# A hybrid decoder layer on one core: slots claimed early for the last w2 weights, two w_ob blocks between w_oa blocks, and FFN b's first weights in weight tiles

## The chip, the cores and the metric

The kernel runs on one core of a Trainium2 chip. Its metric is the time of one execution on the device in microseconds, less is better. Before the change it was 2166.63 us, the median of 3 runs (2165.53 to 2170.79).

## The reference

One layer of a decoder runs over 1056 token rows (1024 of a prompt, 32 of eight samples), model width 1024, hidden width 2816, all in float32:

```
h = layer_norm(ALPHA * x + 0.5 * swiglu(x, f1_w1, f1_w3, f1_w2), ln1_g, ln1_b)
z = h @ w_in + b_in
...
att = combine_groups(outs, lses).astype(h.dtype)
yb, vrows = sgu_branch(uv, sgu_ln_g, sgu_ln_b, sgu_ws, sgu_b)
mix = (jax.nn.sigmoid(ga) * (att @ w_oa) + jax.nn.sigmoid(gb) * (yb @ w_ob)) @ w_out
h = layer_norm(ALPHA * h + mix, ln2_g, ln2_b)
h = layer_norm(ALPHA * h + 0.5 * swiglu(h, f2_w1, f2_w3, f2_w2), ln3_g, ln3_b)
```

`swiglu(x, w1, w3, w2)` is `(silu(x @ w1) * (x @ w3)) @ w2`. `att` (256 wide) comes from three groups of windowed attention, `yb` (512 wide) from a gated chunk mixing. The two FFNs are called FFN a and FFN b below.

## The kernel before, in words

**Products.** Every matrix product is made of TensorE matmuls of 128x128 weights by 264 tokens (four token chunks c of 264 make 1056). A float32 value is split into a high part, a copy that ScalarE casts (L250), and a low part, the difference that VectorE takes (L251); `mm3` issues three matmuls for each 128-deep step (high by high, high by low, low by high), all at L239. Results stand in PSUM in two kinds of tiles, "mm" (three buffers) and "ax" (five). A product may start only when VectorE has taken the result of the product that held its tile before: of an mm tile, that is the third product ahead. Taking it is called evacuation here.

**Weights.** `unit` (L214 on) fetches a weight block of 128x1024 into a raw tile R (L218; two buffers), casts and splits it into two tiles, from the weight pool W (eight buffers) or, with slot=True, from the general pool of S tiles (37 slots). `narrow` does the same for a half or quarter block, both parts in one W tile. Behind each fetch stands a copy of a piece of state from DRAM to DRAM (L211), on the same queue, SyncE's. The order of the instructions is found by a scheduler that runs through the program text with priorities; what comes into a pool's tile later waits until its former content has been read for the last time.

**The end of an FFN.** Most of an FFN's hidden blocks run through Strassen-like sums with seven products; the last part, `out`, walks over g = 0..2 and np = 0..3 with blocks of w2, each prepared by `prep` (L376): it fetches two raw tiles, then yields between steps in which sums of the blocks are formed and split; the last step takes two S tiles, h34 and l34 (L402). A `held` tile (L103) is an S tile that is claimed at once by a one-column copy on GpSimd (L107). During the last block (`final`), each of the seven products calls `fetch`, which loads the hidden blocks of four "plain" blocks, already split, from DRAM scratch (partA or partB, L762, eight tiles of 128x1056), and `W2` collects the fetched w2 units for them. Then the plain products follow, per output block n and token chunk c: twelve matmuls each (L920 is the evacuation), with layer norm steps between (L527 to L549 the centring, L588 to L598 the squares, L626 the scaling, L539 and L540 sums for the mean).

**mix.** After attention, `local(n)` makes w_ob block n: four products of twelve matmuls, each result multiplied into the gate `mt[n]` (L1577). All eight run first. Then eight w_oa blocks: four products of six matmuls each, multiplied into `ta[n]` (also L1577), `mt[n] += ta[n]` over all tokens (L1685), and a split of the sum. Beside blocks 2, 4 and 5 one more gate block of matmuls runs on TensorE. `column_sums` runs between on VectorE (L1643).

**From mix into FFN b.** The w_out products (blocks 3 to 7 for each of four chunks, evacuated at L1702) are followed by a layer norm whose result is written to scratch hD (L643) and split into the operands of FFN b. FFN b starts with plain hidden blocks; for i = 2, `plain` holds two of them. The two units of the first are fetched at c == 2 into S slots, the units of the second when FFN b begins, into W tiles.

Of the kernel before, what the change touches and what calls it, by code (L numbers as in the profile page):

```python
# [13 lines left out]
F32R = mybir.dt.float32r  # L14
# [7 lines left out]
P = 128  # L22
# [11 lines left out]
NG = SEVEN // GP  # L34
HP = GP * P
ORDER = (1, 2, 6, 7, 5, 4, 3)
PLAIN = (0, 19, 20, 21)
NPL = len(PLAIN)
NW = 2
# [30 lines left out]
NLEAD = 6  # L70
NTAIL = 10
LAST = 3
BESIDE = {2: 13, 4: 14, 5: 15}
CHUNKED = 3
SPLIT = [*QKV, 22, 23, 24, 25, 18, 19, 20, 21, *GATES[NLEAD : 16 - NTAIL]]
# [5 lines left out]
class Trunk:  # L81
# [285 lines left out]
    def prep(self, src, f, H, engine):  # L367

        nc = self.nc
        lo, hi, n = slice(0, H), slice(H, 2 * H), 2 * H  # L370
        with self.tc.high_priority(offset=URGENT):
            ab, cd = self.R([P, D])[:, :n], self.R([P, D])[:, :n]
            nc.sync.dma_start(ab, src[1])
            dma = nc.sync.dma_start(cd, src[0])
        self.copy_state(dma, 2)
        tt = engine.tensor_tensor  # L376
        ah, al = self.W([P, D]), self.W([P, D])
        self.split(ah[:, :n], al[:, :n], ab)
        yield
        s12 = self.Q([P, D])  # L380
        tt(s12[:, lo], cd[:, lo], cd[:, hi], op=ALU.add)  # L381
        tt(s12[:, hi], s12[:, lo], ab[:, lo], op=ALU.subtract)  # L382
        yield
        s34 = self.Q([P, D])
        h12, l12 = self.W([P, D]), self.W([P, D])
        self.split(h12[:, :n], l12[:, :n], s12[:, :n])
        tt(s34[:, lo], ab[:, lo], cd[:, lo], op=ALU.subtract)
        yield
        tt(s34[:, hi], ab[:, hi], s12[:, hi], op=ALU.subtract)  # L389
        part = lambda h, l, o=0: [((h, l), o + k * P) for k in range(H // P)]  # L390
        if n == D:
            dd = self.S([P, D], F32R)
            self.split(dd[:, lo], dd[:, hi], cd[:, hi])
            p4 = part(dd[:, lo], dd[:, hi])
        else:
            p4 = []
            for h, l, w in ((ah, al, D - n), (h12, l12, H - (D - n))):
                o = H + len(p4) * P
                self.split(h[:, n : n + w], l[:, n : n + w], cd[:, o : o + w])
                p4 += part(h, l, n)[: w // P]  # L400
        yield
        h34, l34 = self.S([P, D], F32R), self.S([P, D], F32R)  # L402
        self.split(h34[:, :n], l34[:, :n], s34[:, :n])
        self.L[f] = {
            1: part(ah, al), 2: part(ah, al, H), 5: part(h12, l12), 6: part(h12, l12, H),
            7: part(h34, l34), 3: part(h34, l34, H), 4: p4,
        }
        yield
# [260 lines left out]
    def ffn(self, w13, w2p, w2, i, mode, resid):  # L669
# [29 lines left out]
                        next(preps[x] if x == 1 else x, None)  # L699
            self.bg.extend((s0, s1))  # L700
        else:
            units, s1 = self.early
            lns, self.lns = self.lns, {}
            self.drain(lns[NC - 2])
            self.step(self.bg, 1)
            lead = [units] + [[self.unit(w13[f, x]) for x in range(2)] for f in plain[1:]]
            begin(1)
            for c in range(NC):
                self.drain(lns.pop(c))
# [3 lines left out]
                for f, u in zip(plain, lead):  # L713
                    self.hidden8(u, f, c)
                    if c:
                        with self.chained():
                            next(preps[1], None)
            lead = None
        self.sqs = {}
        self.Y = self.A = None  # L720
        loads = deque(self.load_sums(resid))
# [838 lines left out]
    def mix(self):  # L1560
# [99 lines left out]
        self.sums = sums = column_sums()  # L1660
        self.slow.append(sums)
        wbs = deque([self.narrow(a["wo"][0, :, 2 * P :], 4 * P)])
        for n in range(KB):
            local(n)
        was = deque([self.narrow(a["wo"][0, :, : 2 * P], 2 * P)])
        self.yb = None
        ta = [self.fetch_z(26 + n) for n in range(3)]
        while self.bg or self.mid or self.slow[0] is not sums:
            self.tick(1, 1 if self.slow[0] is not sums else 0)
# [3 lines left out]
        for n in range(KB):  # L1673
            wa = was.popleft()
            if n + 1 < KB:
                was.append(self.narrow(a["wo"][n + 1, :, : 2 * P], 2 * P))
            if n + 3 < KB:
                m = NLEAD + NTAIL - KB + n + 3
                ta.append(kept[m] if m in kept else self.fetch_z(29 + n))
            if 26 + n in LATE_GATES:  # L1680
                nc.scalar.activation(ta[n], ta[n], AF.Sigmoid)
            for c in range(NC):
                product(wa, att, c, ta[n])
                self.tick(0, 1)
            nc.vector.tensor_tensor(mt[n], mt[n], ta[n], op=ALU.add)  # L1685
            m2.append((self.S([P, NT], F32R), self.S([P, NT], F32R)))
            self.split(*m2[n], mt[n])
            done += 1
            if n in BESIDE:
                gate(BESIDE[n], NC - 1, 0, 0)  # L1690
        units = kept = self.A = None
        self.sqs, self.lns = {}, {}
        self.Y = self.new_Y(self.hD[0])

# [21 lines left out]
                    centers.append(self.center(c, hs, REST))  # L1716
                    self.mid.append(centers[c])
        ws = [self.unit(a["wout"][n], slot=n < KB - 4) for n in range(half, KB)]
        self.T, self.L = ({}, {}), {}
        self.normed = [None] * NC  # L1720
        for c in range(NC):
            self.drain(centers[c])
# [2 lines left out]
                self.square_step(c, n)  # L1725
            for n in range(half, KB):
                block(ws[n - half], n, c)
            self.start_ln(c, 1, "spill")
            if c == 2:
                units = [self.unit(a["w13b"][0, x], slot=True) for x in range(2)]  # L1730
                self.drain(self.lns[1])
                self.slow.append(self.spread(0, self.Y, self.normed, nc.vector))
        hs = self.hs = None
        self.A = self.normed
        self.early = units, self.spread(1, self.Y, self.normed, nc.vector)

    def run(self):
        a = self.a
# [159 lines left out]
```

## Time and profile before

| what | value |
|---|---|
| median of 3 runs | 2166.63 us |
| the profiled execution | 2166.3 us, of which the span is 2164.2 us |
| mean granted TensorE clock | 0.995 of full speed |
| TensorE busy | 2126.6 us of the span |
| VectorE busy | 1551.9 us |
| ScalarE busy | 889.0 us |
| GpSimd busy | 325.2 us |

In a row of a timeline stand the start, the duration, the engine (PE is TensorE, DVE VectorE, ACT ScalarE, SP SyncE and its DMA queue), the line, the operation, the output and the inputs by pool name, the shape, and how many such instructions the row joins; in brackets how long the engine had been idle before it, and what ended that. The end of a matmul is modelled, so the time lost at a wait is better read from start to start, less the products between. A row of the stretches shows the stretch and its length, then the busy time of PE, PEld, DVE, ACT and POOL with the number of instructions, the granted clock, the DMA share and GB/s.

### The profile page before, as it was taken

How to read it: one execution, taken by the hardware profiler on the slowest of the kernel's cores; microseconds unless marked ns; L12 is line 12 of the kernel's file. 1: busy time of each engine (PE TensorE's matmuls, PEld its weight loads, DVE VectorE, ACT ScalarE, POOL GpSimd, SP SyncE). 2: the span in 40 equal slices, each digit the busy share in tenths (PEclk: the TensorE clock that was granted, in tenths of full speed). 3: DMA queues.
4: the chain of work that ended last, by engine and by line, in shares of the span. 5: the costliest groups of instructions: out<-in, count | busy, mean ns of one | idle time of the engine just before them, and what ended most of it. 6: DMA issues, size and time to landing. Idle time of an engine off the chain costs nothing.

```text
span 2164.2 us, 43247 instructions
## 1 busy us (share of the span) xinstructions
PE 2126.6 (98%) x17307; PEld 2087.7 (96%) x17307; DVE 1551.9 (72%) x2727; ACT 889.0 (41%) x1680; POOL 325.2 (15%) x245
## 2 busy tenths in 40 slices
PE   9999999999999999999999999999999999999997
PEld 8999999999998999999998889999999999999997
DVE  8777777746788835787766658778667777657887
ACT  5444444421224634434475543255444444421224
POOL 0432332200000012222000000000223233100000
PEclk9999999999999999999999999999999999999998
DMA  4445545598875335666865665424444554596852
GB/s 160 146 137 165 190 156 169 202 345 316 330 275 192 130 114 174 208 227 207 289 215 165 217 191 173 154 86 133 138 169 155 189 165 160 192 408 267 305 189 81
DMA packets 168377, 426.51 MB, mean 197 GB/s; under 512 B 24352, under 2 KB 59792, under 8 KB 165488
## 3 DMA queue, kind: packets, MB, share of 16 engines
q1 hardware_dynamic: 167744, 423.21, 56.1%
q8 instruction: 135, 2.21, 0.4%
q14 instruction: 66, 0.54, 0.1%
q10 hardware_dynamic: 432, 0.54, 0.1%
HBM read 304.31 MB, written 165.57 MB: 217 GB/s over the span
## 4 chain that ended last, share of the span: by engine, by line
PE 89%; DVE 5%; DMA 4%; ACT 1%; issue 1%; POOL 0%; SPq 0%; ACTq 0%; DVEq 0%; POOLq 0%
PE ax L239 47%; PE mm L239 38%; PE ax L1201 1%; DMA S<-zD 1%; PE ax L1248 1%; PE ax L1225 1%; DVE W L251 1%; DVE S L251 1%; DMA S<-cD 0%; DMA M<-kv 0%; DVE S L1577 0%; DMA R<-wz 0%; DVE S L626 0%; DMA R<-w2a 0%; PE ax L1543 0%
## 5 line engine op out<-in xcount | busy, mean ns | idle before, releaser
L239 PE MATMUL ax<-S,W 128*128 128x264 f32 x5400 | 706.6, 284 | 1.8 <-ACT S L1029 1.5
L239 PE MATMUL mm<-S,W 128*128 128x264 f32 x5208 | 693.5, 287 | 13.6 <-DVE S L1577 4.1
L239 PEld LDWEIGHTS mm<-S,W 128*128 128x128 f32 x5208 | 655.2, 189 | 27.6 <-issue 8.5
L239 PEld LDWEIGHTS ax<-S,W 128*128 128x128 f32 x5400 | 676.5, 188 | 4.6 <-ACT S L1029 3.0
L239 PE MATMUL ax<-S,S 128*128 128x264 f32 x3240 | 475.7, 284 | 1.6 <-ACT S L1029 1.1
L239 PEld LDWEIGHTS ax<-S,S 128*128 128x128 f32 x3240 | 427.8, 188 | 2.3 <-ACT S L1029 1.3
L239 PE MATMUL mm<-S,S 128*128 128x264 f32 x2472 | 385.2, 286 | 2.6 <-DVE S L251 2.0
L239 PEld LDWEIGHTS mm<-S,S 128*128 128x128 f32 x2472 | 335.1, 189 | 4.3 <-DVE S L251 2.2
L250 ACT CAST W<-R 128x1024 fp32r<-128x1024 f32 (+3 forms) x173 | 128.6, 761 | 317.3 <-PE mm L239 149.9
L381 POOL TENSOR_TENSOR Q<-R 128x512 f32<-128x512 f32 x49 | 73.4, 1498 | 794.1 <-DMA R<-wz 176.8
L251 DVE TENSOR_TENSOR W<-R,W 128x1024 fp32r<-128x1024 f32 (+3 forms) x173 | 156.5, 908 | 23.9 <-ACT W L250 22.9
L250 ACT CAST W<-Q 128x1024 fp32r<-128x1024 f32 (+1 forms) x78 | 76.8, 985 | 213.9 <-POOL Q L382 86.8
L815 DVE SCALAR_TENSOR_TENSOR S<-ax,S 128x264 f32<-128x264 f32 x240 | 99.4, 427 | 66.9 <-PE ax L239 66.5
L456 DVE TENSOR_TENSOR S<-ax,M 128x264 f32<-128x264 f32 x82 | 32.6, 432 | 149.2 <-PE ax L239 149.2
L251 DVE TENSOR_TENSOR S<-Q,S 128x1024 fp32r<-128x1024 f32 (+1 forms) x78 | 108.5, 1391 | 3.8 <-ACT S L250 3.8
L251 DVE TENSOR_TENSOR W<-Q,W 128x1024 fp32r<-128x1024 f32 (+1 forms) x78 | 89.9, 1153 | 27.2 <-ACT W L250 27.2
L250 ACT CAST S<-Q 128x1024 fp32r<-128x1024 f32 (+1 forms) x78 | 76.7, 984 | 68.3 <-PE ax L239 49.8
L107 POOL CAST S<-ones 128x1 fp32r<-128x1 f32 x32 | 17.6, 570 | 487.2 <-PE mm L239 307.7
L250 ACT CAST S<-R 128x512 fp32r<-128x512 f32 (+1 forms) x64 | 44.0, 688 | 110.4 <-DMA sumsB<-S 40.2
L251 DVE TENSOR_TENSOR S<-S,M 128x528 fp32r<-128x528 f32 x72 | 84.5, 1174 | 2.6 <-ACT M L250 0.8
L389 POOL TENSOR_TENSOR Q<-R,Q 128x512 f32<-128x512 f32 x49 | 79.9, 1630 | 1.1
L382 POOL TENSOR_TENSOR Q<-Q,R 128x512 f32<-128x512 f32 x49 | 78.8, 1609 | 2.7
(209 smaller groups left out, 2052.4 us busy)
## 6 DMA issues: line engine op xcount, KB each, us to landing
ws<-st SPq DMA_DIRECT2D x144, 256.0 KB
S<-sumsA SPq DMA_DIRECT2D x63, 528.0 KB
S<-sumsB SPq DMA_DIRECT2D x63, 528.0 KB
M<-kv SPq DMA_DIRECT2D x96, 256.0 KB
sumsA<-M SPq DMA_DIRECT2D x90, 264.0 KB
sumsB<-M SPq DMA_DIRECT2D x90, 264.0 KB
R<-w13b SPq DMA_DIRECT2D x44, 512.0 KB
R<-w13a SPq DMA_DIRECT2D x42, 512.0 KB
```

The costliest lines, as they stand in the source:

```text
L107: self.nc.gpsimd.tensor_copy(t[:, 0, :1] if len(shape) == 3 else t[:, :1], self.ones[:, :1])
L239: mm = lambda a, b, s, e: nc.tensor.matmul(o, a[:, cc], b, start=s, stop=e, skip_group_check=True)
L250: a = self.nc.scalar.copy(hi, src)
L251: b = self.nc.vector.tensor_tensor(lo, src, hi.bitcast(F32), op=ALU.subtract)
L381: tt(s12[:, lo], cd[:, lo], cd[:, hi], op=ALU.add)
L382: tt(s12[:, hi], s12[:, lo], ab[:, lo], op=ALU.subtract)
L389: tt(s34[:, hi], ab[:, hi], s12[:, hi], op=ALU.subtract)
L456: go(one, 5, False, lambda x: tt(h[:, x, 1], one[x], p7[:, x], op=ALU.add))
L815: nc.vector.scalar_tensor_tensor(y(x, r, e), bank[x], HALF, y(x, r, e), op0=ALU.mult, op1=ALU.add)
L1201: nc.tensor.matmul(pS[h][:, r, :nk], q[e, i * P : (i + 1) * P], k[e, k0 : k0 + nk], start=True, stop=True)
L1225: nc.tensor.transpose(pT[r][:, h, o], s[:, r, h, o], self.ident)
L1248: nc.tensor.matmul(pv[0][e, (i % 4) * P : (i % 4 + 1) * P], V[:, i - (nb - 1) + b, e], sT[:, r, h, b * P : b * P + P], start=b == 0, stop= ...
```

## The change

Four edits. `LASTW2` names the last w2 block of an FFN; for it h34 and l34 are held tiles, claimed at the first step of `prep`, no longer S tiles taken at the last. In `mix` only the first six w_ob blocks run ahead of the w_oa blocks, and blocks 6 and 7 follow behind w_oa blocks 0 and 1. FFN b's first two units are fetched in chunk 3, at output blocks 4 and 5, into W tiles, no longer at c == 2 into slots, and those of the second plain block right behind them. `self.yb` is let go behind the last w_oa block, and `self.early` once FFN b's plain blocks are done.

```
+LASTW2 = FB + NG * (KB // 2) - 1
...
+EARLY = 6
...
         self.split(ah[:, :n], al[:, :n], ab)
+        if f == LASTW2:
+            h34, l34 = self.held([P, D], F32R), self.held([P, D], F32R)
         yield
...
-        h34, l34 = self.S([P, D], F32R), self.S([P, D], F32R)
+        if f != LASTW2:
+            h34, l34 = self.S([P, D], F32R), self.S([P, D], F32R)
...
-            units, s1 = self.early
+            lead, s1 = self.early
             lns, self.lns = self.lns, {}
             self.drain(lns[NC - 2])
             self.step(self.bg, 1)
-            lead = [units] + [[self.unit(w13[f, x]) for x in range(2)] for f in plain[1:]]
             begin(1)
...
-            lead = None
+            lead = self.early = None
...
-        for n in range(KB):
+        for n in range(EARLY):
             local(n)
         was = deque([self.narrow(a["wo"][0, :, : 2 * P], 2 * P)])
-        self.yb = None
...
             done += 1
+            if EARLY + n < KB:
+                local(EARLY + n)
             if n in BESIDE:
                 gate(BESIDE[n], NC - 1, 0, 0)
-        units = kept = self.A = None
+        units = kept = self.A = self.yb = None
...
-        self.T, self.L = ({}, {}), {}
+        self.T, self.L, lead = ({}, {}), {}, []
...
                 block(ws[n - half], n, c)
+                if c == NC - 1 and n in (4, 5):
+                    lead.append(self.unit(a["w13b"][PLAIN[0], len(lead)]))
             self.start_ln(c, 1, "spill")
             if c == 2:
-                units = [self.unit(a["w13b"][0, x], slot=True) for x in range(2)]
                 self.drain(self.lns[1])
                 self.slow.append(self.spread(0, self.Y, self.normed, nc.vector))
...
-        self.early = units, self.spread(1, self.Y, self.normed, nc.vector)
+        lead = [lead, [self.unit(a["w13b"][PLAIN[1], x]) for x in range(2)]]
+        self.early = lead, self.spread(1, self.Y, self.normed, nc.vector)
```

The line numbers of the changed kernel are 2 to 5 higher (L918 is then L922, L920 L924, L549 L554, L251 L253, L1577 L1581). How instructions move is shown at three places. A name such as S903 is a tile; the number behind the underscore only counts.

First SyncE's queue at the end of FFN a. S903 to S916 are the eight tiles of the plain hidden blocks, R917 and on the raw tiles of w2. Before:

```order
L863 DMA partA31_97<-M863_7366 128x528
L218 DMA R917_7866<-w2a 128x1024
L218 DMA R920_7915<-w2a 128x1024
L762 DMA S903_7742<-partA00_90 128x1056
L762 DMA S904_7743<-partA01_91 128x1056
L762 DMA S911_7772<-partA10_92 128x1056
L762 DMA S912_7773<-partA11_93 128x1056
L762 DMA S913_7796<-partA20_94 128x1056
L762 DMA S914_7797<-partA21_95 128x1056
L762 DMA S915_7820<-partA30_96 128x1056
L762 DMA S916_7821<-partA31_97 128x1056
L211 DMA ws2<-st2 16x4096 x2
```

And after the change:

```order
L867 DMA partA31_97<-M863_7366 128x528
L766 DMA S912_7775<-partA11_93 128x1056
L766 DMA S913_7798<-partA20_94 128x1056
L766 DMA S914_7799<-partA21_95 128x1056
L766 DMA S915_7822<-partA30_96 128x1056
L220 DMA R917_7868<-w2a 128x1024
L766 DMA S916_7823<-partA31_97 128x1056
L220 DMA R920_7917<-w2a 128x1024
L213 DMA ws2<-st2 16x4096 x2
L220 DMA R929_7950<-w2a 128x1024
L213 DMA ws2<-st2 16x4096
L220 DMA R936_7993<-w2a 128x1024
```

Seven of the eight loads (three of them, S903, S904 and S911, stand further up, behind the write of partA20) now come ahead of the w2 fetches.

Second VectorE at the same place. mm928, mm932 and so on are the plain products in their order on TensorE; S931 and S938 are the low parts of the w2 units from R929 and R936, S978 that of the unit behind them. Before:

```order
L920 SCALAR_TENSOR_TENSOR S609_5361<-mm928_7934,S609_5361 128x264
L920 SCALAR_TENSOR_TENSOR S609_5361<-mm932_7955,S609_5361 128x264
L920 SCALAR_TENSOR_TENSOR S609_5361<-mm934_7971,S609_5361 128x264
L527 TENSOR_TENSOR M900_7676<-M900_7676,S637_5582 128x528
L549 TENSOR_TENSOR S609_5361<-S609_5361,ax933_7969 128x528 x2
L549 TENSOR_TENSOR S636_5554<-S636_5554,ax933_7969 128x528 x2
L251 TENSOR_TENSOR S931_7950<-R929_7948,S930_7949 128x1024
L920 SCALAR_TENSOR_TENSOR S609_5361<-mm939_7998,S609_5361 128x264
```

And after:

```order
L924 SCALAR_TENSOR_TENSOR S609_5361<-mm928_7936,S609_5361 128x264
L253 TENSOR_TENSOR S931_7952<-R929_7950,S930_7951 128x1024
L924 SCALAR_TENSOR_TENSOR S609_5361<-mm932_7957,S609_5361 128x264
L924 SCALAR_TENSOR_TENSOR S609_5361<-mm934_7973,S609_5361 128x264
L554 TENSOR_TENSOR S609_5361<-S609_5361,ax933_7971 128x528
L253 TENSOR_TENSOR S938_7995<-R936_7993,S937_7994 128x1024
L532 TENSOR_TENSOR M900_7678<-M900_7678,S637_5582 128x528
L554 TENSOR_TENSOR S609_5361<-S609_5361,ax933_7971 128x528
L554 TENSOR_TENSOR S636_5554<-S636_5554,ax933_7971 128x528 x2
L253 TENSOR_TENSOR S978_8283<-R976_8281,S977_8282 128x1024
L924 SCALAR_TENSOR_TENSOR S609_5361<-mm939_8000,S609_5361 128x264
```

The split of S931 moved up to right behind mm928's evacuation, and those of S938 and S978 now stand ahead of the evacuation of mm939, no longer behind it.

Third VectorE in the mix, between the first w_oa blocks. Before, where w_oa block 2 follows block 1 (mm1909 to mm1912 belong to block 1, mm1917 to mm1921 to block 2; S1905 and S1914 are low parts of sums):

```order
L1577 TENSOR_TENSOR S1890_15844<-S1890_15844,mm1912_15942 128x264
L251 TENSOR_TENSOR W1916_15956<-R1915_15955,W1916_15956 128x256
L1685 TENSOR_TENSOR S1774_14895<-S1774_14895,S1890_15844 128x1056
L251 TENSOR_TENSOR S1905_15906<-S1773_14893,S1904_15905 128x1056
L1577 TENSOR_TENSOR S1891_15846<-S1891_15846,mm1917_15962 128x264
L1643 TENSOR_REDUCE X1863_15602<-Q1902_15894 128x8
L1577 TENSOR_TENSOR S1891_15846<-S1891_15846,mm1919_15973 128x264
L1577 TENSOR_TENSOR S1891_15846<-S1891_15846,mm1920_15981 128x264
L251 TENSOR_TENSOR S1914_15952<-S1774_14895,S1913_15951 128x1056
L1577 TENSOR_TENSOR S1891_15846<-S1891_15846,mm1921_15989 128x264
```

And after, at the same place, with w_ob block 7 (mm1911 to mm1914) between w_oa block 1 (up to mm1908) and block 2:

```order
L1581 TENSOR_TENSOR S1879_15723<-S1879_15723,mm1908_15887 128x264
L253 TENSOR_TENSOR W1902_15852<-R1901_15851,W1902_15852 128x256
L1688 TENSOR_TENSOR S1774_14897<-S1774_14897,S1879_15723 128x1056
L1581 TENSOR_TENSOR S1838_15375<-S1838_15375,mm1911_15901 128x264
L1581 TENSOR_TENSOR S1838_15375<-S1838_15375,mm1912_15915 128x264
L253 TENSOR_TENSOR S1910_15897<-S1774_14897,S1909_15896 128x1056
L1581 TENSOR_TENSOR S1838_15375<-S1838_15375,mm1913_15929 128x264
L1581 TENSOR_TENSOR S1838_15375<-S1838_15375,mm1914_15943 128x264
L253 TENSOR_TENSOR W1916_15958<-R1915_15957,W1916_15958 128x256
L1581 TENSOR_TENSOR S1880_15725<-S1880_15725,mm1917_15964 128x264
L1647 TENSOR_REDUCE X1863_15604<-Q1907_15885 128x8
L1581 TENSOR_TENSOR S1880_15725<-S1880_15725,mm1919_15975 128x264
```

Block 1's sum over all tokens (L1685, then L1688) and a split of a block's sum stood back to back ahead of mm1917's evacuation; now evacuations of w_ob block 7 stand between and behind them.

## The prediction

> **What bounds the kernel.** I read the page's busy times first, then its chain of waits, then TensorE's timeline at every place that the change touches. All of it is one profiled execution of 2166.3 us (span 2164.2 us, 2.1 us around it), 0.3 us under the median of 2166.63 us. A difference of 0.3%, 6.5 us, is about what a measurement of this kernel can tell from no change, so faster begins at 2160.1 us.
>
> ```profile
> PE 2126.6 (98%) x17307; PEld 2087.7 (96%) x17307; DVE 1551.9 (72%) x2727; ACT 889.0 (41%) x1680; POOL 325.2 (15%) x245
> PE 89%; DVE 5%; DMA 4%; ACT 1%; issue 1%; POOL 0%; SPq 0%; ACTq 0%; DVEq 0%; POOLq 0%
> ```
>
> TensorE is busy 98% of the span and carries 89% of the chain. The change adds no matmul and removes none; it can only win back time in which TensorE waits or runs slowly. So I walk through its waits at the three touched stages and lay the new order over them with the old durations.
>
> **Part (a), the end of FFN a: the old loss.** TensorE's timeline there:
>
> ```profile
> 657.73 2.66 PE L239 MATMUL mm<-S,W 128*128 128x264 f32 x18
> 660.78 0.75 PE L239 MATMUL mm<-S,S 128*128 128x264 f32 x4 [0.39 <-ACT S L250]
> 663.54 5.69 PE L239 MATMUL mm<-S,S 128*128 128x264 f32 x32 [2.02 <-DVE S L251]
> 669.07 0.61 PE L543 MATMUL ax<-M,ones 128*128 128x264 f32 x2
> 669.32 1.82 PE L239 MATMUL mm<-S,S 128*128 128x264 f32 x12
> 670.99 3.09 PE L239 MATMUL mm<-S,W 128*128 128x264 f32 x24
> 676.17 3.18 PE L239 MATMUL mm<-S,W 128*128 128x264 f32 x24 [2.10 <-DVE S L920]
> 679.19 1.14 PE L239 MATMUL mm<-S,S 128*128 128x264 f32 x8
> 1296.84 23.61 PE L239 MATMUL mm<-S,W 128*128 128x264 f32 x192 [0.82 <-DVE S L251]
> ```
>
> The last row is from the mix, an undisturbed run: 192 products in 23.61 us, the last one's modelled end included, so one takes 0.122 us. From 657.73 to 679.19 are 21.46 us with 18+4+32+2+12+24+24 = 116 products, 14.15 us. The loss is **7.3 us**. The brackets show 4.5 of it; the rest is that each wait costs some 0.2 more than shown (ends are modelled) and that the row of 32 takes 5.69 us instead of 3.9. The stretches tell why:
>
> ```profile
> 660.73:664.14 3.41, 1.35 (x9) 1.14 (x10) 3.41 (x7) 2.15 (x5) 0.00 (x0) 1.00 0.01 6
> 664.14:667.55 3.41, 3.41 (x18) 3.41 (x17) 2.47 (x5) 0.39 (x2) 0.00 (x0) 0.50 0.87 249
> 674.38:677.79 3.41, 1.62 (x13) 1.62 (x14) 3.41 (x9) 1.54 (x3) 0.00 (x0) 1.00 0.49 191
> 1322.92:1326.33 3.41, 1.80 (x13) 1.38 (x12) 3.41 (x7) 1.69 (x2) 0.00 (x0) 1.00 0.67 249
> 1326.33:1329.74 3.41, 3.41 (x17) 3.41 (x17) 3.04 (x5) 0.76 (x2) 0.00 (x0) 0.50 0.12 35
> ```
>
> Column 3 is TensorE's busy time, the first number behind POOL the granted clock. Behind a stretch of 3.41 us in which TensorE was busy 1.35 us, and behind one of 1.80 us, the next one was granted half the clock; half of 3.41 us, **1.7 us**, is lost each time. The stretch with 1.62 us busy, the one of the 2.10 us wait, was not: the row at 676.17 runs at full pace (3.02 us to the next for 24). So a stretch idle by half, even in several short waits, can cost a halved one, but does not always.
>
> The Trainium skill ("TensorE: Matmul & The Clock Gate", section "Part 1: The HAM clock gate") has TensorE fall to half rate after at least one idle window of about 3.4 us, free-running. The trace agrees on 3.41 us and the half; it does not agree that the whole window must be idle, since no wait shown is longer than 2.10 us. By the page no new short wait below would halve the clock, and the sum would keep all its gain there; by the rows it can (first rival).
>
> **(a), the new order.** The early claim brings the eight part loads ahead of the w2 fetches and the last w2 units with them, so that TensorE's products mm928 to mm942 find their operands. I take no TensorE work away, so mm939 still ends at 660.4 (660.78 less the wait), mm928 at 655.9, mm934 at 658.9. What ends last then is VectorE, whose old rows give the prices:
>
> ```profile
> 658.17 1.11 DVE L920 SCALAR_TENSOR_TENSOR S<-mm,S 128x264 f32<-128x264 f32 x3 [2.47 <-PE mm L239]
> 659.20 0.70 DVE L527 TENSOR_TENSOR M<-M,S 128x528 f32<-128x528 f32 x1
> 659.82 2.54 DVE L549 TENSOR_TENSOR S<-S,ax 128x528 f32<-128x528 f32 x4
> 662.27 1.22 DVE L251 TENSOR_TENSOR S<-R,S 128x1024 fp32r<-128x1024 f32 x1
> 663.41 0.42 DVE L920 SCALAR_TENSOR_TENSOR S<-mm,S 128x264 f32<-128x264 f32 x1
> 669.65 0.33 SPq L218 DMA_DIRECT2D R<-wzp  x1
> 677.67 1.22 DVE L251 TENSOR_TENSOR W<-R,W 128x1024 fp32r<-128x1024 f32 x1
> ```
>
> From start to start an evacuation takes 0.34 us, L527 0.62, four L549 2.45, a split 1.14. In the new order, between mm934's evacuation (done at 659.3) and the end of mm939's stand four L549, L527, two splits and that evacuation: 2.45+0.62+2.28+0.34 = 5.7, so 665.0. mm947, which takes mm939's PSUM buffer, is due three products of 12 behind 658.9, at 663.3. It waits 1.7, with the 0.2 and the margin **2.2 us**. The second wait is mm965's, for mm955's evacuation, ahead of which stands the split of a unit whose fetch goes out when S978's split has freed the raw tile (664.6). The last two rows are this fetch and this split in the old order: 8.0 us apart. The split then starts at 672.6, the evacuation is done at 674.2, and mm965 is due at 672.5: **2.0 us** with the 0.2. A third wait, mm968's, I put at 0.5. So (a) wins 7.3-2.2-2.0-0.5 = **2.6 us**. Bounds: if the split of S978 needs those 8.0 us too, it starts at 665.5, 2 us later, and one halved stretch may come back: 2.6-2.0-1.7 = -1.1, a loss. If the fetch of the second takes 3.5 us as below, that wait falls to 1.0: 3.6. GpSimd's two more one-column copies hide at its 15%.
>
> **Part (b), the mix.** The old loss:
>
> ```profile
> 1321.01 2.45 PE L239 MATMUL mm<-S,W 128*128 128x264 f32 x18 [0.56 <-ACT W L250]
> 1324.61 1.01 PE L239 MATMUL mm<-S,W 128*128 128x264 f32 x6 [1.15 <-DVE S L1577]
> 1326.08 8.39 PE L239 MATMUL mm<-S,W 128*128 128x264 f32 x54 [0.46 <-DVE S L1577]
> 1334.64 1.00 PE L239 MATMUL mm<-S,W 128*128 128x264 f32 x6 [0.17 <-DVE S L1577]
> ```
>
> From 1296.84 to 1334.64 are 37.80 us with 192+18+6+54 = 270 products, 32.94 us: **4.9 us** lost, a halved stretch of 1.7 among it. VectorE's groups over 1290 to 1340:
>
> ```profile
> L1577 DVE TENSOR_TENSOR S<-S,mm 128x264 f32<-128x264 f32 x38 | 15.7, 423 | 8.1 <-PE mm L239 8.0
> L1685 DVE TENSOR_TENSOR S<-S,S 128x1056 f32<-128x1056 f32 x5 | 6.3, 1251 | 0.0
> L1643 DVE TENSOR_REDUCE X<-Q 128x8 f32<-128x1024 f32 x5 | 6.0, 1210 | 0.0
> L251 DVE TENSOR_TENSOR S<-S,S 128x1056 fp32r<-128x1056 f32 x3 | 3.7, 1249 | 0.0
> L251 DVE TENSOR_TENSOR W<-R,W 128x256 fp32r<-128x256 f32 x8 | 3.4, 419 | 1.8 <-ACT W L250 1.8
> ```
>
> A w_oa block needs four L1577, one L1685, the split of its sum and a weight split, 4x0.42+1.25+1.25+0.42 = 4.6 us of VectorE, against 24 products, 2.9 us of TensorE: VectorE falls behind there, and L1643 adds to it. A w_ob block is 48 products, 5.9 us, with four L1577 and one weight split, 2.1 us. Two of them between the first w_oa blocks give VectorE 7.6 us to catch up. In the new order the sum and the split behind w_oa block 1 fall among w_ob block 7's products, and the waits of 0.56, 1.15 and 0.46 and the halved stretch go. What is late next: the first w_oa block, whose weight tile is free only when the w_ob products of the block before have read it, 0.6 us; a wait like the old 0.46 at block 3, 0.4; and one where the last w_oa blocks follow each other without cover, 1.0. So **(b)** wins 4.9-0.6-0.4-1.0 = **2.9 us**. Bounds: if VectorE's arrears only meet a later block with a halved stretch, 2.9-1.7 = 1.2; if only the first wait stands, 4.3.
>
> **Part (c), into FFN b.** TensorE, and the row that it waits for:
>
> ```profile
> 1458.57 0.45 PE L239 MATMUL mm<-S,W 128*128 128x264 f32 x2
> 1460.57 2.68 PE L239 MATMUL mm<-S,W 128*128 128x264 f32 x20 [1.54 <-DVE W L251]
> 1451.00 0.33 SPq L218 DMA_DIRECT2D R<-w13b  x1
> 1454.47 1.05 ACT L250 CAST W<-R 128x1024 fp32r<-128x1024 f32 x1 [3.35 <-DMA R<-w13b]
> 1459.30 1.22 DVE L251 TENSOR_TENSOR W<-R,W 128x1024 fp32r<-128x1024 f32 x1
> ```
>
> From 1458.57 to 1460.57 two products ran: 2.00-0.24 = 1.7 us lost to the second unit's split at 1459.30. With the first plain block's units fetched in the last output blocks, the pair behind it goes out some 3 to 4 us earlier than 1451.00, and its splits end near 1457, ahead of 1458.6. **(c)** wins **1.7 us**; nothing if VectorE, which has no gap there, still puts the split last. What is moved besides: the writes of hD come behind these fetches, hidden, since they are read only at the end of FFN b; and four W tiles are held until FFN b's first plain block is done, so the next units' casts come later, with several microseconds to spare by the order (last rival).
>
> **Part (d), the end of FFN b**, where the same early claim works.
>
> ```profile
> 2122.31 4.13 PE L239 MATMUL mm<-S,W 128*128 128x264 f32 x31
> 2127.67 1.71 PE L239 MATMUL mm<-S,W 128*128 128x264 f32 x12 [1.22 <-DVE S L920]
> ```
>
> 5.36 us for 31 products (3.78) lose 1.6. In the new order the evacuation awaited stands ahead of four 128x1056 operations, and the next one behind them: a new wait of 0.8. **(d)** wins **0.8 us** (0 to 1.6).
>
> **The sum.** 2.6+2.9+1.7+0.8 = 8.0 us off 2166.3 is 2158.3; at the median, 2166.6-8.0 = **2158.6 us**. The bounds of the terms added give 0.1 to 11.4. All missing at once is unlikely, so the forecast's own range is 2155.5 to 2161.5.
>
> **Rivals.** First: the two new waits of some 2 us at the end of FFN a halve the clock. For it: the stretches with 1.35 and 1.80 us busy; against: the one with 1.62 did not halve it, and a wait of 2 us can fall across two stretches. Once gives 2160.3, twice 2162.0 us. 0.24.
>
> Second: the halved stretches do not hang on these waits, and both stay. For it: only three stretches decide, and a free-running window falls elsewhere in a shifted run; against: both halvings stood right behind the emptiest stretch. 2158.6+3.4 = 2162.0 us. The page's rule, by which such short waits explain no halving, would come out here. 0.08.
>
> Third: (a)'s lead is lost to a later chain. Behind it the chain goes through DMAs (4% of it, 87 us), whose time an earlier TensorE does not move. 2158.6+2.6 = 2161.2 us. 0.08.
>
> Fourth: VectorE is the bound at (a) and (b), and the order only moves its arrears. It was busy all of 3.41 us in three of the five stretches; against it, 72% over the span and the cover counted above. Only (c) and (d) are left: 2166.6-2.5 = 2164.1 us. 0.10.
>
> Fifth, slower: FFN b's weight tiles. Four of eight are held by plain blocks, and if only one of the rest is free for the next pair, units follow each other serially: fetch 3.5 (1451.00 to 1454.47), cast 1.05, split 1.22, 5.8 us for a unit against 24 products, 2.9 us. Each is 2.9 late; it turns slower than before from three such units on, and five give 14.5 us: 2158.6+14.5 = 2173.1 us. Against it: raw tiles are fetched ahead of the free weight tile. 0.05.
>
> **Numbers.** The forecast has 0.45. Its range lies by four fifths below 2160.1 us, 0.36; two fifths of the first rival (once halved, with terms a little better) and pieces of the second and third add 0.14: faster 0.50. Same 0.44: the rest of those and the fourth. Slower 0.06: the fifth and the sum of all losses. The range, from 2154.5 (the terms at their better bounds, less one) to 2165.2 (the fourth rival with (d) at nothing), leaves out the fifth and the tails.
>
> **What would show it.** At the end of FFN a: no wait for L250 or L251 between the plain products, waits of about 2 us ending on the evacuations of mm939 and mm955, and a clock of 1.00 throughout; 0.50 there speaks for the first rival. In the mix: mm1917 to mm1921 without wait, full clock, and small waits at the first and the late w_oa blocks. Into FFN b: no wait for a W split. The prediction is wrong if VectorE's waits are no smaller than those they replace, or if FFN b's first blocks wait for weights.

## The result, and the profile after

| | before | after |
|---|---|---|
| median of 6 runs each | 2166.24 us (2163.99 to 2170.79) | 2156.19 us (2152.76 to 2159.24) |
| profiled execution, its span | 2166.3, 2164.2 us | 2158.47, 2156.7 us |
| TensorE busy | 2126.6 us | 2124.5 us |

The ratio of the runs is 0.9945, with a 95% interval of 0.9934 to 0.9956: 11.9 us, 9.5 to 14.3. The medians lie 10.0 us apart. Forecast was 8.0 us. Two later comparisons of the same two kernels gave 0.9959 and 0.9958, 8.9 and 9.1 us (below).

The profiled execution of the changed kernel is one of its longer ones and 7.8 us shorter than that of before. Where the 7.8 us come from can be read by the time at which TensorE starts its N-th matmul, in both traces, each from its first matmul:

| N | program place | before, us | after, us | lead, us |
|---|---|---|---|---|
| 150 | start | 26.15 | 27.26 | -1.11 |
| 5400 | end of FFN a | 677.47 | 676.16 | 1.31 |
| 9900 | before the mix | 1232.41 | 1230.63 | 1.78 |
| 10950 | behind the w_oa blocks | 1371.92 | 1366.93 | 4.99 |
| 11700 | into FFN b | 1465.32 | 1458.37 | 6.96 |
| 17250 | last FFN blocks | 2142.61 | 2135.09 | 7.53 |

From place to place that is 2.4 us at the end of FFN a (forecast 2.6), 3.2 in the mix (2.9), 2.0 into FFN b (1.7) and 0.6 at the end (0.8), and 0.5 between FFN a and the mix, less 1.1 at the start, where nothing was changed. What that 1.1 is comes with the account of the prediction.

TensorE at the end of FFN a, after (rows of its timeline, in the same columns as before):

```profile
658.73 2.31 PE L241 MATMUL mm<-S,W 128*128 128x264 f32 x16
660.87 3.09 PE L241 MATMUL mm<-S,S 128*128 128x264 f32 x24
665.97 4.70 PE L241 MATMUL mm<-S,S 128*128 128x264 f32 x24 [2.00 <-DVE S L924]
670.50 1.64 PE L241 MATMUL mm<-S,W 128*128 128x264 f32 x12
...
676.57 1.73 PE L241 MATMUL mm<-S,W 128*128 128x264 f32 x12 [0.62 <-DVE S L924]
678.13 1.61 PE L241 MATMUL mm<-S,S 128*128 128x264 f32 x12
...
680.54 4.65 PE L241 MATMUL mm<-S,S 128*128 128x264 f32 x36 [0.23 <-DVE S L924]
```

The waits for the splits (0.39 and 2.02) are gone; mm947, the product at 665.97, waits 2.00 us for an evacuation. The row behind it takes 4.70 us for 24 products that elsewhere take 3.1: a halved stretch again. VectorE says why mm947 waits:

```profile
659.60 0.43 DVE L924 SCALAR_TENSOR_TENSOR S<-mm,S 128x264 f32<-128x264 f32 x1 [1.36 <-PE mm L241]
659.95 0.69 DVE L554 TENSOR_TENSOR S<-S,ax 128x528 f32<-128x528 f32 x1
660.56 1.22 DVE L253 TENSOR_TENSOR S<-R,S 128x1024 fp32r<-128x1024 f32 x1
661.70 0.70 DVE L532 TENSOR_TENSOR M<-M,S 128x528 f32<-128x528 f32 x1
662.32 1.92 DVE L554 TENSOR_TENSOR S<-S,ax 128x528 f32<-128x528 f32 x3
664.26 1.23 DVE L253 TENSOR_TENSOR S<-R,S 128x1024 fp32r<-128x1024 f32 x1
665.40 0.42 DVE L924 SCALAR_TENSOR_TENSOR S<-mm,S 128x264 f32<-128x264 f32 x1
```

This is the queue of the forecast, from mm934's evacuation (659.60) to mm939's (665.40), without a gap: 5.8 us from start to start, forecast 5.7.

The mix, the way into FFN b, and the end of FFN b, TensorE:

```profile
1295.44 6.09 PE L241 MATMUL mm<-S,W 128*128 128x264 f32 x48 [0.79 <-DVE S L253]
1302.07 35.27 PE L241 MATMUL mm<-S,W 128*128 128x264 f32 x282 [0.54 <-ACT W L252]
1337.80 19.03 PE L241 MATMUL mm<-S,W 128*128 128x264 f32 x150 [0.46 <-DVE S L1581]
1357.22 5.04 PE L241 MATMUL mm<-S,W 128*128 128x264 f32 x39 [0.38 <-DVE S L1707]
...
1448.38 11.16 PE L241 MATMUL mm<-S,W 128*128 128x264 f32 x90
...
2122.16 4.04 PE L241 MATMUL mm<-S,S 128*128 128x264 f32 x31 [0.47 <-DVE S L924]
```

The first w_oa block waits 0.54 us for its weight tile, and then 282 products run at one pace, 0.125 us each, where five waits (0.56, 1.15, 0.46, 0.17 and 0.46) and a halved stretch stood. Into FFN b nothing waits for weights: 90 products in one row. At the end a wait of 0.47 stands for that of 1.22.

### The profile page after: what moved, and what is told of

It reads as the page before. It is cut to its first block, busy times and chain, and to the rows that moved or that the text cites. A ratio compares the mean times of both kernels' runs of the same rounds, so it can differ in the third digit from the quotient of the medians.

```text
span 2156.7 us, 43261 instructions
## 1 busy us (share of the span) xinstructions
PE 2124.5 (99%) x17307; PEld 2086.6 (97%) x17307; DVE 1552.1 (72%) x2727; ACT 889.5 (41%) x1680; POOL 323.5 (15%) x249
## 4 chain that ended last, share of the span: by engine, by line
PE 85%; DVE 5%; DMA 5%; issue 1%; POOL 1%; ACT 1%; SPq 1%; ACTq 0%; DVEq 0%; POOLq 0%
PE ax L241 44%; PE mm L241 37%; DMA M<-kv 2%; PE ax L1205 1%; DVE W L253 1%; PE ax L1252 1%; DMA R<-wz 1%; PE ax L1229 1%; DVE M L1428 1%; DMA S<-zD 1%; DMA S<-cD 1%; DVE X L1433 0%; DVE S L631 0%; DMA S<-hD 0%; PE ax L620 0%
## 5 line engine op out<-in xcount | busy, mean ns | idle before, releaser
L241 PE MATMUL mm<-S,W 128*128 128x264 f32 x5400 | 715.7, 287 | 7.9 <-ACT S L252 2.6
L241 PEld LDWEIGHTS mm<-S,W 128*128 128x128 f32 x5400 | 677.6, 189 | 21.6 <-issue 8.5
L241 PE MATMUL mm<-S,S 128*128 128x264 f32 x2280 | 359.6, 286 | 2.7 <-DVE S L924 2.7
L241 PEld LDWEIGHTS mm<-S,S 128*128 128x128 f32 x2280 | 311.3, 189 | 4.1 <-ACT M L593 2.2
L252 ACT CAST W<-R 128x256 fp32r<-128x256 f32 (+2 forms) x175 | 130.7, 764 | 309.3 <-PE mm L241 140.1
L253 DVE TENSOR_TENSOR W<-R,W 128x256 fp32r<-128x256 f32 (+2 forms) x175 | 156.8, 899 | 22.4 <-ACT W L252 21.4
L253 DVE TENSOR_TENSOR S<-Q,S 128x1024 fp32r<-128x1024 f32 (+1 forms) x78 | 111.3, 1427 | 5.5 <-ACT S L252 5.4
L253 DVE TENSOR_TENSOR W<-Q,W 128x1024 fp32r<-128x1024 f32 (+1 forms) x78 | 90.3, 1158 | 29.0 <-ACT W L252 28.9
L253 DVE TENSOR_TENSOR S<-S,M 128x528 fp32r<-128x528 f32 x72 | 83.9, 1165 | 3.7 <-ACT M L252 2.4
```

The source lines that it names most:

```text
L241: mm = lambda a, b, s, e: nc.tensor.matmul(o, a[:, cc], b, start=s, stop=e, skip_group_check=True)
L252: a = self.nc.scalar.copy(hi, src)
L253: b = self.nc.vector.tensor_tensor(lo, src, hi.bitcast(F32), op=ALU.subtract)
```

## The experiments

The theory after this reading: each edit gains at its own place, by the waits that it takes away, and the gains add. Its rival: a good part of the time is halved stretches, which fall out anew in each execution. All ratios below are to runs of the kernel before on the same chip, with 95% intervals, and 0.001 is 2.17 us.

**The three edits one by one.** `w2_alone` is the kernel before with the first edit, and no more:

```
+LASTW2 = FB + NG * (KB // 2) - 1
...
+        if f == LASTW2:
+            h34, l34 = self.held([P, D], F32R), self.held([P, D], F32R)
...
-        h34, l34 = self.S([P, D], F32R), self.S([P, D], F32R)
+        if f != LASTW2:
+            h34, l34 = self.S([P, D], F32R), self.S([P, D], F32R)
```

> The kernel before with the early claim for the last w2 block alone. Theory (the gains are those of the three places and add up): 2.4 us at the end of FFN a, with a wait of about 2.0 on the evacuation of mm939 and a halved stretch behind it, and 0.6 at the end of FFN b: 3.0 us faster than before, near 2163.2. Rival (the gain at the median is the number of halved stretches, which falls out anew in every run): no lead at a place that explains the median, and runs that differ by steps of about 1.7 us. Rival (a lead of FFN a is given back in the attention): same as before within 1 us.

Measured 2161.8 us, ratio 0.9978 (0.9968 to 0.9987): 4.8 us, more than the 3.0 of the places. In its profile the mix has the order of before, and nearly the same waits, but no halved stretch:

```profile
1318.35 2.44 PE L240 MATMUL mm<-S,W 128*128 128x264 f32 x18 [0.56 <-ACT W L251]
1321.95 0.99 PE L240 MATMUL mm<-S,W 128*128 128x264 f32 x6 [1.16 <-DVE S L1581]
1323.41 6.81 PE L240 MATMUL mm<-S,W 128*128 128x264 f32 x54 [0.48 <-DVE S L1581]
1330.42 0.99 PE L240 MATMUL mm<-S,W 128*128 128x264 f32 x6 [0.19 <-DVE S L1581]
```

54 products take 6.81 us here and took 8.39 in the trace of before. The waits do not change that much; where the stretches begin does.

`wob_alone` is the kernel before with the second edit alone: `EARLY = 6` and its two places in `mix`.

> The kernel before with two w_ob blocks between w_oa blocks alone. Theory of places: 3.6 us between 1296 and 1337 us, by no wait at w_oa block 2 and no halved stretch there, so 3.6 faster, near 2162.6. Rival of halved stretches: in the mix the halved stretch returns in another place, and 1.9 faster or less. Rival of VectorE's arrears: the waits move to the last w_oa blocks, under 1 us faster.

Measured 2164.53 us, 0.9994 (0.9985 to 1.0003): 1.3 us, -0.7 to 3.3, less than the 3.6 expected. In its trace the mix gains 3.6 us (lead -1.63 us at N = 10350, 1.95 at 10650), so the place did what it should; but some 1.6 of these are the halved stretch (54 products in 8.39 us against 6.81), which the old order does not have there in every profile. And it paid more at the end of FFN a, in the old order:

```profile
671.26 3.17 PE L240 MATMUL mm<-S,W 128*128 128x264 f32 x24 [0.42 <-DVE S L921]
677.79 5.65 PE L240 MATMUL mm<-S,W 128*128 128x264 f32 x24 [3.35 <-DVE S L921]
```

`lead_alone` is the kernel before with FFN b's first units as in the changed kernel. Of its edit, the lines that move the fetches:

```
+                if c == NC - 1 and n in (4, 5):
+                    lead.append(self.unit(a["w13b"][PLAIN[0], len(lead)]))
...
-                units = [self.unit(a["w13b"][0, x], slot=True) for x in range(2)]
```

> The kernel before with FFN b's first weights in weight tiles alone. Theory of places: the 1.54 us wait at 1460 us goes and nothing takes its place, 1.8 to 2.0 us faster, near 2164.4. Rival (weight tiles run serially in FFN b): waits for W splits behind 1465 us, same or slower.

Measured 2166.21 us, 0.9996 (0.9987 to 1.0006): 0.9 us, -1.3 to 2.8. The trace shows the gain at its place (lead 0.12 at N = 10950, 2.07 at 11700), of which 1.61 are left at 17250, and TensorE waits for no W split behind 1465 us: the rival of serial weight tiles falls.

`all_again`, the changed kernel unaltered:

> The changed kernel once more. Theory of places: the sum of the three parts, 3.0+3.6+1.9 = 8.5 us, 2157.7, with leads of 2.4, 3.6, 1.9 and 0.6 at the same places. Rival of halved stretches: the profile shows other halved stretches than the first (7.7 to 15.4 us, 666 to 670 us and the end from 2144 us on), and the median is 10 us faster or more where the one at 666 us stays out in most runs.

Measured 2158.52 us, 0.9959 (0.9943 to 0.9975): 8.9 us. The three alone make 7.0 us, within the intervals of the sum. In its trace mm947 waits 1.90 us (2.00 in the first profile), and no stretch is halved there; another is, at 1002 us, in a stage that no edit touches.

**One edit left out.** `no_w2`, `no_wob` and `no_lead` are the changed kernel without the first, second and third edit. `all_third` is the changed kernel beside the latter two.

> The changed kernel a third time, beside the next three on one chip. Theory: 9 us faster than before (mean over all its runs so far), mean clock about 0.996 to before's 0.995.

> The changed kernel without the second edit: all eight w_ob blocks first. Theory: the waits of 0.56, 1.15 and 0.46 return at the first w_oa blocks, 1.9 us by the order and a halved stretch in a part of the runs: 2 to 3.6 us slower than the changed kernel. Rival (alone it won 1.3 to 2.8 us at the median; half of it is clock): 1.3 us slower.

> The changed kernel without the third edit: FFN b's first units in slots again. Theory: the 1.5 us wait for a W split at 1460 us returns, 1.7 us slower than the changed kernel. Rival (alone it won 0.7 to 1.1 us at the median, since time is given back behind): 0.7 us slower.

> The changed kernel without the first edit (no early claim in either FFN). Theory (the early claim is worth more than its places' waits, since the old order there had a halved stretch or two in each of four profiles and the new one in about every second): 5 us slower than the changed kernel, 4 faster than before, mean clock as before's 0.995. Rival (the terms as forecast, 3.4): 3.4 slower than the changed kernel, 5.7 faster than before.

| label | median, us | ratio to before | worth of the edit left out, us |
|---|---|---|---|
| all_third | 2158.03 | 0.9958 (0.9945 to 0.9972) | |
| no_wob | 2160.51 | 0.9970 (0.9959 to 0.9980) | 2.6 |
| no_lead | 2160.37 | 0.9971 (0.9961 to 0.9981) | 2.8 |
| no_w2 | 2161.49 | 0.9976 (0.9966 to 0.9987) | 3.9 |

The last column is the difference to 0.9958, and good to some 3.5 us, so it does not tell a theory from its rival. Together 9.3 us, against 9.1 for the whole. In `no_lead` the wait for the W split is back at its place, though 1.19 us long and not 1.54:

```profile
1454.32 4.81 PE L241 MATMUL mm<-S,W 128*128 128x264 f32 x36 [1.19 <-DVE W L253]
```

**Which FFN the early claim pays in.** `claim_b_only` and `claim_a_only` make the held tiles depend on the FFN:

```
+        if f == LASTW2 and self.second:
...
+        if f != LASTW2 or not self.second:
...
+        nc, preps, self.second = self.nc, {}, i != 0
```

`claim_a_only` has `i == 0` in the last line.

> The changed kernel with the early claim in FFN b alone, FFN a as before. Theory of places: at the end of FFN a the old waits for L252, L253 and L924 return (0.39, 2.02, 2.10) and 2.4 us with them by 700 us; the end of FFN b keeps its 0.5 us wait in place of 1.22. Rival (the early claim matters little in FFN a, the rest is clock): no loss by 700 us but for halved stretches.

> The changed kernel with the early claim in FFN a alone. Theory: 0.6 us slower than the changed kernel, its wait of 1.22 us at the end of FFN b back, mean clock 0.996. Rival (FFN b's claim carries a larger share of the first edit's 5 us): 1.5 us slower or more.

`claim_b_only`, one execution, took 2163.69 us; at N = 5400 it stands 3.9 us behind the changed kernel's profile, with the old waits back and two halved stretches:

```profile
661.05 0.75 PE L241 MATMUL mm<-S,S 128*128 128x264 f32 x4 [0.26 <-ACT S L252]
663.96 4.16 PE L241 MATMUL mm<-S,S 128*128 128x264 f32 x32 [2.16 <-DVE S L253]
...
676.55 5.65 PE L241 MATMUL mm<-S,W 128*128 128x264 f32 x24 [3.06 <-DVE S L924]
```

`claim_a_only` has 2157.97 us, 0.9958 (0.9946 to 0.9971), the same as the whole: the end of FFN b is worth less than can be told. Its trace has the wait of 1.25 us back there. So the first edit pays in FFN a.

**How much cover.** `early_7` and `early_5` put one and three w_ob blocks between the w_oa blocks, by `EARLY = 7` and `EARLY = 5`.

> The changed kernel with one w_ob block between w_oa blocks in place of two. Theory (a w_ob block is cover for VectorE's arrears, 5.9 us of products with 2.1 us of VectorE): half of the cover, so waits of about 1 us in all return at w_oa blocks 2 or 3; 1 to 1.5 us slower than the changed kernel, 2158 to 2159. Rival (one block is enough): same.

> The changed kernel with three w_ob blocks between w_oa blocks. Theory of cover: the waits that stand at 1337.8 and 1357.2 (0.46 and 0.38) shrink by half, 0.4 us faster, not to be told from no change. Rival (slots: mt and ta tiles of more blocks are held at once, so later loads come later): new waits on DMA in the w_out blocks, 1 us or more slower.

`early_7`: 2160.45 us, 0.9970 (0.9959 to 0.9982), 2.6 us slower than the whole by the ratios, which is inside their intervals. In its trace the waits return one block later, as expected:

```profile
1324.01 1.00 PE L241 MATMUL mm<-S,W 128*128 128x264 f32 x6 [0.33 <-DVE S L1581]
1325.48 6.81 PE L241 MATMUL mm<-S,W 128*128 128x264 f32 x54 [0.46 <-DVE S L1581]
1332.48 0.99 PE L241 MATMUL mm<-S,W 128*128 128x264 f32 x6 [0.19 <-DVE S L1581]
1333.94 6.86 PE L241 MATMUL mm<-S,W 128*128 128x264 f32 x54 [0.48 <-DVE S L1581]
```

`early_5`: 2160.32 us, 0.9976 (0.9967 to 0.9985), 3.9 us slower than the whole, by waits that neither theory had. No wait on a DMA turned up; in its trace the first w_oa block waits for its weight tile twice as long, another 0.60 us is lost at 1332, and the two waits that were to shrink by half have grown to 0.52 and 0.87:

```profile
1294.33 1.00 PE L241 MATMUL mm<-S,W 128*128 128x264 f32 x6 [1.12 <-ACT W L252]
1295.76 11.36 PE L241 MATMUL mm<-S,W 128*128 128x264 f32 x90 [0.43 <-DVE W L253]
1307.48 23.99 PE L241 MATMUL mm<-S,W 128*128 128x264 f32 x192 [0.36 <-DVE S L1581]
1332.07 5.37 PE L241 MATMUL mm<-S,W 128*128 128x264 f32 x42 [0.60 <-DVE S L1581]
1337.96 19.01 PE L241 MATMUL mm<-S,W 128*128 128x264 f32 x150 [0.52 <-DVE S L1581]
1357.85 4.39 PE L241 MATMUL mm<-S,W 128*128 128x264 f32 x34 [0.87 <-DVE S L1707]
```

From N = 9900, ahead of the mix, to 11700 that costs 1.5 us against the changed kernel's profile (`early_7`: 1.9). Why the rest of the 3.9 is lost stays open. Six early blocks are the best of the three by these traces and by the ratios, though the difference to seven is not clear of their intervals.

**The wait that is left.** `split_behind` fetches the unit behind the last w2 unit one product later, so that its split comes behind mm939's evacuation:

```
+                if mode != "out" and c == 0 and n == 3:
+                    with self.fenced():
+                        self.early = [self.unit(self.a["wzp"][0], slot=True, ahead=AFTER)]
...
-                    self.early = [self.unit(self.a["wzp"][n], slot=True, ahead=AFTER) for n in range(CHUNKED)]
+                    self.early += [self.unit(self.a["wzp"][n], slot=True, ahead=AFTER) for n in range(1, CHUNKED)]
```

> The changed kernel with one move: the split of the unit behind the last w2 unit (S978) goes behind the evacuation of mm939, no longer ahead of it. Theory (the wait of 2.00 us at mm947 is VectorE's queue, 1.14 us of it this split): the wait falls to 0.9 or less, the halved stretch behind it stays out, the wait of 0.62 at mm965 stays under 1: 1 us by the order and up to 1.7 more where the stretch would have been halved, so 1 to 2.5 us faster than the changed kernel, near 2155.5. Rival (a free-running window decides alone, whatever the waits): the order's 1.1 us, and the same mean clock as the changed kernel's. Rival (the split is only late elsewhere): the wait turns up at mm949 or mm965, no change.

> The changed kernel with S978's split behind mm939's evacuation, now beside the changed kernel. In its first profile the wait at mm947 was 0.77 for 2.00, that at mm965 1.30 for 0.62, and no stretch was halved at the end of FFN a. Theory (the emptiest stretch decides on the halving): 0.6 us by the order and some 1 us by stretches that are not halved, 1 to 2 us faster than the changed kernel, and a higher mean clock. Rival (the wait moved on to mm965): same within 0.6 us.

The order did what was wanted: the queue of VectorE ahead of mm939's evacuation is one split shorter, and the wait fell from 2.00 to 0.77 us, while mm965's rose to 1.30:

```profile
660.93 1.93 DVE L554 TENSOR_TENSOR S<-S,ax 128x528 f32<-128x528 f32 x3
662.77 0.43 DVE L924 SCALAR_TENSOR_TENSOR S<-mm,S 128x264 f32<-128x264 f32 x1
663.12 1.22 DVE L253 TENSOR_TENSOR S<-R,S 128x1024 fp32r<-128x1024 f32 x1
```

```profile
663.35 3.46 PE L241 MATMUL mm<-S,S 128*128 128x264 f32 x24 [0.77 <-DVE S L924]
...
673.06 1.72 PE L241 MATMUL mm<-S,W 128*128 128x264 f32 x12 [1.30 <-DVE S L924]
```

Measured 2155.99 us, 0.9958 (0.9946 to 0.9971), and beside the changed kernel 2155.26 to its 2158.03 us, ratios 0.9955 (0.9942 to 0.9967) and 0.9958. Both its spans in a profile were 2152 us, and neither has a halved stretch at the end of FFN a. It is the fastest by the medians, but the ratios do not tell it from the changed kernel.

**Where halved stretches come from.** The granted clocks of 16 profiles (both kernels' and the 14 runs) show it. In each profile all halved stretches begin on one grid of 3.4133 us: in `w2_alone` at 8.08, 666.86, 939.92 and 2148.24 us, of which the middle two lie 80 steps apart, and all four leave 1.25 to 1.26 us over whole steps. From profile to profile the grid is shifted (1.07 us in that of the changed kernel, 2.68 in `all_third`). So I counted the matmuls that start in each stretch of the grid, from 30 to 2120 us; a full one holds 28 (stretches that are halved themselves are left out):

| matmuls started in a stretch | followed by a halved one | not |
|---|---|---|
| 10 or fewer | 12 | 0 |
| 11 or 12 | 7 | 10 |
| 13 or more | 0 | all others, 9731 |

Here are stretches, within 0.06 us of the grid, of three profiles, each with the one behind it, in the columns of the prediction: the changed kernel and `all_third` with mm947's wait (2.00 and 1.90 us), and `wob_alone` with that of 3.35.

```profile
663.28:666.69 3.41, 1.41 (x12) 1.22 (x11) 3.39 (x7) 2.31 (x5) 0.00 (x0) 1.00 0.59 214
666.69:670.10 3.41, 3.41 (x18) 3.41 (x17) 3.41 (x7) 1.69 (x5) 0.00 (x0) 0.50 0.79 267
```

```profile
661.50:664.91 3.41, 1.51 (x14) 1.33 (x12) 3.41 (x6) 2.30 (x5) 0.00 (x0) 1.00 0.73 235
664.91:668.32 3.41, 3.41 (x28) 3.41 (x29) 3.41 (x7) 1.70 (x4) 0.00 (x0) 1.00 0.72 231
```

```profile
673.68:677.09 3.41, 0.76 (x7) 0.55 (x5) 3.41 (x5) 0.00 (x0) 0.00 (x0) 1.00 0.91 299
677.09:680.50 3.41, 2.71 (x12) 2.71 (x13) 3.41 (x8) 2.00 (x4) 0.00 (x0) 0.51 0.09 35
```

The counts in these rows include matmuls that reach in from the stretch ahead. A wait of 2 us is on the border. Where the grid cut 0.3 us or more off mm947's, 13 or 14 matmuls started in the stretch with the rest of it (`no_lead`, `claim_a_only`), and nothing was halved. Where one stretch held nearly all of it, 10 to 12 did, and the next stretch was halved in some profiles (the changed kernel's with 10, `early_5` with 11), and not in others (`all_third` with 11). What decides at 11 or 12 stays open. At the end of FFN a the old order had 7 halved stretches in 5 profiles, the new one 4 in 9, `split_behind` none in 2. In the first w_oa blocks the old order had 3 in 4, the new one, with one to three blocks between, none in 12.

**What a halved stretch costs.** At the end of FFN a it was 0.4 us in the new order, not 1.7. Behind mm947 stands mm965, which waits for VectorE too. Without a halved stretch this second wait is long; here is `all_third`:

```profile
664.88 3.16 PE L241 MATMUL mm<-S,S 128*128 128x264 f32 x24 [1.90 <-DVE S L924]
675.06 1.72 PE L241 MATMUL mm<-S,W 128*128 128x264 f32 x12 [1.75 <-DVE S L924]
```

From mm947 to mm965 that is 10.18 us, as in the four other new-order profiles without a halved stretch there, with 1.70 to 1.75 us of wait at mm965. In the four with one it is 10.58 to 10.60 us, with 0.62 of wait: VectorE gains while TensorE is slow, and the second wait takes up most of the loss. The whole place, from the start of matmul 5100 to that of 5700, takes:

| order at the end of FFN a | profiles | us |
|---|---|---|
| old | `before`, `no_w2`, `lead_alone`, `claim_b_only`, `wob_alone` | 81.39, 81.39, 82.76, 84.09, 84.55 |
| new, no stretch halved there | `all_again`, `all_third`, `claim_a_only`, `no_lead`, `no_wob` | 78.42 to 78.48 |
| new, one halved | `after`, `w2_alone`, `early_7`, `early_5` | 78.88 to 79.40 |
| `split_behind` | its two | 77.08, 77.31 |

In the mean the old order takes 82.84 us and the new one 78.72, 4.1 less. `split_behind` gains another 1.5 us at the place, which is within what it was expected to gain and less than the ratios can tell. In its two traces no 3.41 us at the end of FFN a, wherever the grid may fall, hold fewer than 15 starts; in the five of the new order without a halved stretch, 9 or 10 are the fewest.

## Why the prediction was right or wrong

**What failed is the size of (a)**, 2.6 us in the sum. In the traces it is 4.1 us in the mean, and 2.4 between the two first ones; the edit came out at 4.8 us alone and 3.9 inside, where 3.4 were forecast with FFN b. The new order was forecast well: the 81.39 us of the profile before, less 2.6, are 78.8, and the new order's mean is 78.7. The queue ahead of mm947 was right to 0.1 us; mm965's wait, put at 2.0 by an old fetch of 8.0 us, was 1.70 to 1.75 where nothing was halved; the third wait was 0.2 for 0.5. The mis-sized step is the old loss of 7.3 us. I read it from one execution, which with `no_w2`'s is the fastest of the old order's five; their mean loses 1.4 us more, with waits of up to 3.35 us and 1.4 halved stretches (7 in 5) where that one had 2.10 us and one.

The step about the clock was half right. One short wait can halve it, as the first rival had it, and did in 4 of 9 profiles; but the price of 1.7 us for it was wrong here, where it cost 0.4.

**(b)** was forecast at 2.9 us and measured at 1.3 alone and 2.6 inside; from N = 9900 to 10950 it is 3.3 us in the mean of the traces (four of the old order, ten of the new one with two blocks). The first wait was as forecast (0.54 for 0.6); the small one at block 3 did not come; one of 0.46 and one of 0.38 stand behind. Cover was the right reason: with one block waits of the old kind come back, one block later.

**(c)** was forecast at 1.7 and measured at 0.9 alone and 2.8 inside; from N = 10950 to 11700 it is 1.8 us in the mean of the traces (four and twelve). Whether the earlier fetches or the weight tiles take the wait away, no run tells apart. The fifth rival, slower by serial weight tiles, found nothing: TensorE waits for no W split in FFN b. **(d)** had a new wait of 0.47 for the 0.8 forecast; from N = 11700 to 17250 it is 0.9 us in the mean of the traces (five and eleven), for 0.8, and too small to time by the runs.

**The rivals.** The first came in part of the executions, at a smaller price. The second named the right cause for its half, a free-running window; but that both halved stretches stay was wrong: the emptiest stretches went with the waits. The Trainium skill ("TensorE: Matmul & The Clock Gate", section "Part 1: The HAM clock gate") calls the window free-running and the result different from run to run: the grids agree, with 1.07, 1.26 and 2.68 us. That at least a whole window must be idle does not agree: 12 of 12 stretches with up to 10 of 28 matmuls were followed by half the clock. The third rival, the lead lost to DMAs, did not show in the first profile, where 1.31 us at N = 5400 was 1.78 at 9900. Over all traces the way from N = 5700 to 9900 takes 515.1 to 518.0 us behind the old order and 513.2 to 519.4 behind the new, in the mean 0.5 us more, so a small part may be given back; this scatter does not tell. The fourth fell: the mix kept its gain.

**The sum and the range.** With the sizes of the traces the sum is 4.1+3.3+1.8+0.9 = 10.1 us, for 8.0 forecast, and the three comparisons gave 11.9, 8.9 and 9.1, in the mean 10.0. On 2166.24 us their ratios are 2154.3, 2157.4 and 2157.1 us; the first lies just under the lower end of the range, 2154.5. I built that range from the bounds of the terms of one execution (the better bounds add to 11.2, not 11.4, and the fourth rival with (d) at nothing gives 2164.9, not 2165.2, which changes little). No term stood for the difference between executions: 77 runs of the kernel before went from 2160.75 to 2172.12 us. By their granted clock:

| mean granted clock | runs | mean, us |
|---|---|---|
| 0.993 | 3 | 2170.2 |
| 0.994 | 27 | 2168.0 |
| 0.995 | 32 | 2166.2 |
| 0.996 | 13 | 2164.1 |
| 0.997 | 2 | 2166.3 |

Up to 0.996 some 2 us go with each step of 0.001, which is 2.2 us of the span; the two runs at 0.997 do not follow. This scatter is in every comparison of six runs. The profiled execution of the changed kernel had two halved stretches at the start where that of before had one, and so began 1.1 us behind. That the 11.9 us of the first comparison against 8.9 and 9.1 are no more than this scatter fits the intervals, but was not shown apart.

## What to carry to other kernels

Where a kernel keeps one engine busy to 98%, walk the queue of the engine that releases it in the new order, with old durations: the wait of 2.0 us and its place came out of that to 0.2 us. But read the old loss from more than one execution: one trace put it 1.4 us too low, and that was most of the error. Work without much evacuation, put between blocks that need much of it, is cover, but more of it need not be better: with three blocks the first w_oa block waited 1.12 us for its weight tile, with two 0.54. And price a wait by where it can fall on the clock's grid, not by whether the old trace happened to show a halved stretch behind it, and a halved stretch by the wait that follows it.

## What the runs showed of the hardware

In these traces the clock goes by fixed stretches of 3.41 us whose start differs from execution to execution: in 16 profiles half the clock always followed a stretch in which 10 or fewer of 28 matmuls started, sometimes one with 11 or 12, never one with 13 or more. So one wait of 2.0 us risks half the clock, and two of 0.8 and 1.3 ten microseconds apart (`split_behind`) did not. And a halved stretch need not be paid in full: behind mm947, where another wait for VectorE follows, it cost 0.4 us and not 1.7.
